# Cross-covariance attention on one core: the Gram norms read before the K^T Q copy, and fp32 transposes in place of fp32 identity matmuls

## The chip, the cores and the metric

The kernel runs on one core of a Trainium2 chip. The metric is the device time of one execution in microseconds (us). The core has five engines that run their own instruction streams and meet at semaphores: TensorE (PE, whose weight loads the profile lists apart as PEld), VectorE (DVE), ScalarE (ACT), GpSimd (POOL) and SyncE (SP, which here only issues DMAs).

## The reference, cut to what matters

```python
# Q, K, V: [8, 12, 512, 64] float32, seeded random
Q_norm = Q / (norm(Q, axis=-2) + 1e-10)       # norm over the 512 rows, per column
K_norm = K / (norm(K, axis=-2) + 1e-10)
attn = einsum('bhnd,bhne->bhde', Q_norm, K_norm)      # 64 x 64 per head
attn = softmax(attn, axis=-1)
out = einsum('bhnd,bhde->bhne', V, attn)
```

For each of the 96 heads, a 64x64 matrix Q^T K is formed, scaled by the column norms of Q and K, put through a softmax, and V is multiplied by its transpose.

## The kernel before

The 96 heads are taken in 24 units of four heads (`HU = 4`). A unit's Q, K and V are tiles of 128 partitions x 1024 floats (512 KB each); head h has the 32 partitions 32h to 32h+31, and each partition holds 16 rows of 64. All loads and stores are issued by SyncE in one queue, in the order of the program.

The scheduling is manual: each engine executes its instructions in the order in which the Python code issues them. The main loop runs over 27 steps `s`, and in a step different pieces work on different units, so that the chain of one unit stretches over four steps:

- `cast_q`, `cast_k` (VectorE, L74 and L77) turn Q and K of unit s+1 to bf16 side by side in `qkb`.
- `grams(s)` (TensorE, L88) multiplies `qkb` with itself: 16 row slices x 4 heads = 64 matmuls of 32 rows, accumulated in `gbuf`, one PSUM bank per head. A head's 128x128 result holds Q^T Q, K^T K and the two cross products.
- `keep_kq(s)` (ScalarE, L93) copies K^T Q (partitions 64 to 127, columns 0 to 63 of each of the four banks) to SBUF.
- `norms(s)` (VectorE, L100) takes the diagonal of each bank with a mask and a sum, four operations; GpSimd (L105) raises the four numbers per partition to the power -1/2, giving `rq`.
- `scale_k(s-1)` (VectorE, L110) scales the rows of K^T Q by the K norms into `kqs`; `logits(s-1)` (TensorE, L116) turns the four 64x64 fp32 blocks by a matmul against the identity; `scale_q(s-1)` (VectorE, L120) scales by the Q norms into `sl`; `exps(s-1)` (ScalarE, L124) and `normalise` (VectorE, L128 to L132, one step later) finish the softmax into a bf16 buffer `ab`.
- `cast_v(s-2)` (ScalarE, L81) and `vtrans(s-2)` (TensorE, L138, eight bf16 transposes; ScalarE copy L140) turn V into `vt`; `doubled(s-2)` (TensorE L145, ScalarE copy L146) puts a second copy of `ab` on the upper partitions.
- `outs(s-3)` (TensorE, L156: 32 matmuls; ScalarE, L160: two copies `so`) forms the output.

Two accesses of one PSUM bank by two engines are put one after the other by the framework: it makes the later one in program order wait for the earlier. So the order of `keep_kq` and `norms`, which read the same four banks, decides which of the two waits. The logits and the doubled attention share one bank as well (`ltile`), and `logits(s-1)` waits for the ScalarE copy of `doubled(s-2)`.

The buffers that matter: `gbuf` is single, so `grams(s+1)` may start when all readers of `grams(s)` are done; `po` has two buffers; Q, K and V tiles have five each. Stores lag by six steps (`STORE_LAG = 6`).

Of the kernel before, what the change touches and what calls it, by code (L numbers as in the profile page):

```python
# [14 lines left out]
D = 64  # L15
# [7 lines left out]
def kernel(  # L23
# [7 lines left out]
    nc = tc.nc  # L31
# [25 lines left out]
    qf, kf, vf, vb, qkb, nsq, rq, kqs, sl, ex, vt, so, kq = ({} for _ in range(13))  # L57
# [55 lines left out]

    def logits(u):
        for h in range(HU):
            nc.tensor.matmul(lg[:, h, :], kqs[u][D:, h, :], ident[D:, D:], tile_position=(D, 0))  # L116

    def scale_q(u):
        s = sl[u] = small.tile([D, HU, D], F32, name="sl")
# [44 lines left out]
    lg = ltile[0:D, 0]  # L164
# [6 lines left out]
    ident = const.tile([128, 128], F32, name="ident")  # L171
# [11 lines left out]
    def on(f, u):  # L183
        if 0 <= u < U:
            f(u)
# [3 lines left out]
    for s in range(U + 3):  # L189
        on(load_qk, s + LOAD_AHEAD)  # L190
        on(load_v, s + V_AHEAD)
        on(store, s - STORE_LAG)
        on(cast_v, s - 2)
        on(cast_q, s + 1)
        on(normalise, s - 2)
        on(scale_k, s - 1)
        on(grams, s)
        on(keep_kq, s)
        on(norms, s)
        on(cast_k, s + 1)  # L200
        on(doubled, s - 2)
        on(outs, s - 3)
        on(logits, s - 1)
        on(scale_q, s - 1)
        on(exps, s - 1)
        on(vtrans, s - 2)
# [32 lines left out]
```

## Time and profile before

| | us |
|---|---|
| median of 3 runs | 146.97 (146.03 to 147.4) |
| the profiled execution, its own time | 146.33 |
| its span, first to last instruction | 144.6 |
| TensorE busy / VectorE busy / ScalarE busy | 105.3 / 93.1 / 99.0 |
| mean granted TensorE clock (1 is full) | 0.767 |

The profile is of one execution. Its parts are: busy time per engine; the span in 40 slices with the clock granted to TensorE and the use of the DMA engines; the DMA queues; the chain of work that ended last, followed back from the last instruction; groups of equal instructions with their mean durations and the idle time ahead of them. In the chain, "issue" is time in which an engine waited for nothing that the profile shows. TensorE records are pipelined, so the duration of one record is longer than the distance to the next.

### The profile page before, as it was taken

The numbers are of one execution on the slowest core, as the hardware profiler recorded it, in microseconds if no ns is written. First come the engines' busy times: TensorE is split into PE (matmuls) and PEld (weight loads), VectorE is DVE, ScalarE is ACT, GpSimd is POOL, SyncE is SP. The second block draws the span as 40 slices with busy tenths as digits, with TensorE's granted clock in tenths as the row PEclk, the third lists the DMA queues.
The fourth block names the chain that finished last, engine by engine and source line by source line (L and its number), as shares of the span: only waits on it lengthen the run. The fifth ranks groups of instructions, "written<-read, shape, count | busy, mean of one in ns | idle before, by whom it ended". The sixth has DMA issues, their size and how long they took to land.

```text
span 144.6 us, 6358 instructions
## 1 busy us (share of the span) xinstructions
PE 105.3 (73%) x2712; PEld 83.4 (58%) x2712; DVE 93.1 (64%) x360; ACT 99.0 (68%) x169; POOL 38.9 (27%) x35
## 2 busy tenths in 40 slices
PE   0347898788999829966496994959699595986630
PEld 0336686566768619754374863848477464965520
DVE  0466979876767766677964777766676975744200
ACT  3011587886687866798866698669497887778960
POOL 6032334313505321413330512320303330320000
PEclk9999999955555985699975589595955998577555
DMA  4999999999999999999999999999999963312333
GB/s 167 402 417 416 404 405 413 399 407 409 416 408 413 419 407 416 413 411 422 406 417 413 415 415 416 419 410 418 411 414 419 381 253 133 150 56 94 145 145 145
DMA packets 13852, 50.73 MB, mean 351 GB/s; under 512 B 1537, under 2 KB 1537, under 8 KB 13825
## 3 DMA queue, kind: packets, MB, share of 16 engines
q1 hardware_dynamic: 13824, 50.34, 86.6%
q8 instruction: 21, 0.34, 1.0%
q14 instruction: 7, 0.05, 0.1%
HBM read 37.75 MB, written 12.58 MB: 348 GB/s over the span
## 4 chain that ended last, share of the span: by engine, by line
PE 56%; DVE 14%; issue 14%; ACT 9%; DMA 3%; ACTq 0%; SPq 0%; DVEq 0%
PE gram L88 23%; PE lgdup L116 11%; PE po L156 10%; PE vps L138 9%; DVE scr L100 6%; PE lgdup L145 4%; DVE qkb L77 4%; DMA kf<-in_K_dram 3%; ACT vb L81 3%; ACT kq L93 2%; ACT vt L140 2%; DVE sl L120 1%; DVE qkb L74 1%; ACT so L160 1%; DVE ab L132 1%
## 5 line engine op out<-in xcount | busy, mean ns | idle before, releaser
L105 POOL TENSOR_TENSOR rq<-nsq,mhalf 128x4 f32<-128x4 f32 x24 | 36.5, 1520 | 89.9 <-DVE nsq L100 89.9
L88 PE MATMUL gram<-qkb 32*128 32x128 bf16 x1536 | 39.7, 270 | 18.7 <-DVE qkb L77 9.3
L88 PEld LDWEIGHTS <-qkb 32*128 32x128 bf16 x1536 | 32.4, 121 | 24.2 <-issue 12.3
L100 DVE CUSTOM_DVE_ANT_0 scr<-gram,ident 128x128 f32<-128x128 f32 x96 | 22.2, 288 | 22.7 <-ACT kq L93 22.6
L160 ACT COPY so<-po 128x512 f32<-128x512 f32 x48 | 26.0, 589 | 6.4 <-PE po L156 5.2
L156 PE MATMUL po<-ab,vt 128*32 128x128 bf16 x768 | 21.1, 264 | 7.5 <-issue 6.3
L156 PEld LDWEIGHTS <-vt 128*32 128x32 bf16 x768 | 15.0, 117 | 17.7 <-issue 8.4
L81 ACT CAST vb<-vf 128x1024 bf16<-128x1024 f32 x24 | 25.1, 1045 | 0.0
L140 ACT COPY vt<-vps 128x1024 bf16<-128x1024 bf16 x24 | 24.0, 1001 | 1.2 <-PE vps L138 0.4
L116 PE MATMUL lgdup<-ident,kqs 64*64 64x64 f32 x192 | 22.3, 279 | 2.6 <-ACT ab L146 2.5
L124 ACT ACTIVATE ex<-sl 64x256 f32<-64x256 f32 x24 | 10.0, 417 | 18.7 <-DVE sl L120 18.7
L116 PEld LDWEIGHTS lgdup<-ident,kqs 64*64 64x64 f32 x192 | 18.4, 184 | 6.7 <-ACT ab L146 4.0
L138 PE MATMUL vps<-identb,vb 128*128 128x128 bf16 x192 | 20.4, 269 | 0.1
L74 DVE CAST qkb<-qf 128x1024 bf16<-128x1024 f32 x24 | 16.3, 677 | 5.0 <-DMA qf<-in_Q_dram 5.0
L93 ACT COPY kq<-gram 64x256 f32<-64x256 f32 x24 | 8.8, 368 | 14.4 <-PE gram L88 13.9
L77 DVE CAST qkb<-kf 128x1024 bf16<-128x1024 f32 x24 | 16.5, 689 | 0.5 <-DMA kf<-in_K_dram 0.5
L138 PEld LDWEIGHTS <-vb 128*128 128x128 bf16 x192 | 14.8, 121 | 2.7 <-issue 0.6
L120 DVE TENSOR_TENSOR sl<-lgdup,rq 64x256 f32<-64x256 f32 x24 | 9.9, 414 | 9.9 <-PE lgdup L116 8.6
L145 PE MATMUL lgdup<-ab,identb 64*64 64x256 bf16 x24 | 8.2, 342 | 5.7 <-DVE ab L132 5.6
L110 DVE TENSOR_TENSOR kqs<-kq,rq 64x256 f32<-64x256 f32 x24 | 10.1, 422 | 1.0 <-POOL rq L105 0.3
L128 DVE TENSOR_REDUCE esum<-ex 64x4 f32<-64x256 f32 x24 | 9.7, 405 | 1.4 <-ACT ex L124 1.4
L132 DVE TENSOR_TENSOR ab<-ex,rinv 64x256 bf16<-64x256 f32 x24 | 10.0, 417 | 0.8
(14 smaller groups left out, 27.6 us busy)
## 6 DMA issues: line engine op xcount, KB each, us to landing
qf<-in_Q_dram SPq DMA_DIRECT2D x24, 512.0 KB, 10.0
kf<-in_K_dram SPq DMA_DIRECT2D x24, 512.0 KB, 10.0
vf<-in_V_dram SPq DMA_DIRECT2D x24, 512.0 KB, 10.1
out_dram<-so SPq DMA_DIRECT2D x24, 512.0 KB, 9.9
```

The lines of the kernel that those rows point to most:

```text
L74: nc.vector.tensor_copy(qkb[u][:, :, 0:D], qf[u])
L77: nc.vector.tensor_copy(qkb[u][:, :, D:], kf[u])
L81: nc.scalar.copy(w.rearrange("p t d -> p (t d)"), vf[u])
L88: nc.tensor.matmul(gbuf[:, h, 0:2 * D], x, x, start=(t == 0), stop=(t == R - 1), tile_position=(NV * h, 0))
L100: nc.vector.tensor_tensor_reduce(out=scr, in0=gbuf[:, h, 0:2 * D], in1=ident, scale=1.0, scalar=1e-20, op0=ALU.mult, op1=ALU.add, accum_ou ...
L105: nc.gpsimd.tensor_tensor(out=r, in0=n2, in1=mhalf, op=ALU.pow)
L116: nc.tensor.matmul(lg[:, h, :], kqs[u][D:, h, :], ident[D:, D:], tile_position=(D, 0))
L138: nc.tensor.transpose(ps[:, t, :], vb[u][:, t, :], identb)
L140: nc.scalar.copy(w, ps)
L145: nc.tensor.matmul(dup[D:], identb[0:D, 0:D], a[0:D, :, 0, :], tile_position=(0, D))
L156: nc.tensor.matmul(po[rows, k, :], vt[u][:, TP // 2 * i + k, rows], a[:, h].rearrange("p a d -> p (a d)"), tile_position=(0, NV * h),)
L160: nc.scalar.copy(s[:, TP // 2 * i:TP // 2 * (i + 1), :], po)
```

## The change

```diff
     def logits(u):
         for h in range(HU):
-            nc.tensor.matmul(lg[:, h, :], kqs[u][D:, h, :], ident[D:, D:], tile_position=(D, 0))
+            nc.tensor.transpose(lg[:, h, :], kqs[u][D:, h, :], ident[D:, D:])
...
         on(grams, s)
-        on(keep_kq, s)
         on(norms, s)
         on(cast_k, s + 1)
         on(doubled, s - 2)
+        on(keep_kq, s)
         on(outs, s - 3)
         on(logits, s - 1)
```

The first hunk gives the four 64x64 turns of a step to TensorE's transpose form: the operands, the place in the array (rows 64 to 127, columns 0 to 63) and the output stay. In the compiled program an fp32 matmul against the identity is two passes, each a weight load and a matmul; a transpose is one. Counted in the compiled programs, TensorE's stream goes from 5,458 instructions to 5,266: eight fewer in each of 24 steps.

The second hunk moves `keep_kq` behind `norms`, `cast_k` and `doubled` in a step. It moves rows on ScalarE alone. In the middle of the program, one step of ScalarE before; `ab_120` is one of the three attention buffers, and the square brackets give the engines waited for:

```order
51 L81 CAST vb<-vf 128x1024 [waits DMAHW2_49,Activation_49]
52 L93 COPY kq<-gram 64x256 [waits PE_49]
53 L146 CAST ab_120<-lgdup 64x4x64 [waits PE_49,Activation_49]
54 L160 COPY so<-po 128x512 [waits PE_49] x2
55 L124 ACTIVATE ex<-sl 64x256 [waits DVE_49]
56 L140 COPY vt<-vps 128x1024 [waits PE_49,Activation_49]
```

And the same step of the changed kernel:

```order
51 L81 CAST vb<-vf 128x1024 [waits DMAHW2_49,Activation_49]
52 L146 CAST ab_120<-lgdup 64x4x64 [waits PE_49,Activation_49]
53 L93 COPY kq<-gram 64x256 [waits DVE_49]
54 L160 COPY so<-po 128x512 [waits PE_49] x2
55 L124 ACTIVATE ex<-sl 64x256 [waits DVE_49]
56 L140 COPY vt<-vps 128x1024 [waits PE_49,Activation_49]
```

The K^T Q copy now stands behind the copy of the doubled attention, and it waits for VectorE's norms in place of TensorE's Gram matmuls. VectorE's rows keep their order; what changes there is the wait of the first norm of a step (one piece of the difference, early in the program):

```order
 L132 TENSOR_TENSOR ab_116<-ex,rinv 64x4x64 [waits DVE_49]
 L110 TENSOR_TENSOR kqs<-kq,rq 64x256 [waits Pool_49]
-L100 ISA scr,nsq<-gram,ident 128x128 [waits Activation_49]
+L100 ISA scr,nsq<-gram,ident 128x128 [waits PE_49]
 L100 ISA nsq 128x1
```

The norms now wait for TensorE alone. TensorE gains a wait: the first Gram matmul of a step now waits for ScalarE, that is for the K^T Q copy of the step before, since that copy is now the last reader of `gbuf`:

```order
 L138 MATMUL vps<-identb,vb 128x128
 L88 LDWEIGHTS qkb [waits DVE_49]
-L88 MATMUL gram<-qkb 128x128
+L88 MATMUL gram<-qkb 128x128 [waits Activation_49]
 L88 LDWEIGHTS qkb
 L88 MATMUL gram<-qkb 128x128
```

The TensorE rows themselves stand in the same order as before.

## The prediction

> **What bounds the kernel now.** I read the page first: the slices and the DMA queues, then the chain by line.
>
> ```profile
> PEclk9999999955555985699975589595955998577555
> DMA  4999999999999999999999999999999963312333
> q8 instruction: 21, 0.34, 1.0%
> PE gram L88 23%; PE lgdup L116 11%; PE po L156 10%; PE vps L138 9%; DVE scr L100 6%; PE lgdup L145 4%; DVE qkb L77 4%; DMA kf<-in_K_dram 3%; ACT vb L81 3%; ACT kq L93 2%; ACT vt L140 2%; DVE sl L120 1%; DVE qkb L74 1%; ACT so L160 1%; DVE a
> ```
>
> The DMA engines are full until about 115 us, yet the waits show that the engines hardly ever wait for data:
>
> ```profile
> DVE qkb L74 <- DMA qf<-in_Q_dram: 5.0, 2, 4.1
> ```
>
> This is the largest wait for a load: two times, 4.1 of its 5.0 us in one of them, at the start. So loads do not set the pace.
>
> Of the span, 14% of the chain is "issue", time in which TensorE waits for nothing that is shown. So I listed the chain in order of time (start, length, what):
>
> ```profile
> 29.28 0.87 PE gram L88 x30
> ...
> 51.93 1.98 issue
> 53.91 0.37 PE po L156 x5
> 54.28 1.04 PE lgdup L116 x8
> 55.32 0.97 PE vps L138 x8
> 56.29 1.82 PE gram L88 x48
> 58.11 0.35 PE lgdup L145
> 58.46 0.98 PE po L156 x29
> ...
> 72.35 0.79 PE gram L88 x42
> ...
> 77.14 1.24 issue
> 78.37 0.93 PE gram L88 x27
> ...
> 115.43 0.97 PE gram L88 x54
> ...
> 118.42 0.56 PE gram L88 x25
> 118.97 1.93 issue
> 120.90 0.73 PE gram L88 x39
> ```
>
> The stops come in the middle of a group of matmuls (after 25 of 64 Gram matmuls, after 27 of 32 output matmuls), where no semaphore stands. The moments at which TensorE **resumes** are what to look at: 29.28, 53.91 (24.63 later, 4 x 6.16), 72.35 (18.44, 3 x 6.15), 78.37 (6.02), 115.43 (37.06, 6 x 6.18), 120.90 (5.47). They beat at about 6.1 us whether the stop is 1.2 or 2.0 us long and whether the clock row stands at 5 or at 9. What lies between two of them is counted by a view of the groups, TensorE alone, from 72.36 to 78.36 us:
>
> ```profile
> L88 PE MATMUL gram<-qkb 32*128 32x128 bf16 x79 | 2.0, 258 | 2.0 <-issue 2.0
> L116 PE MATMUL lgdup<-ident,kqs 64*64 64x64 f32 x8 | 1.1, 318 | 0.0
> L138 PE MATMUL vps<-identb,vb 128*128 128x128 bf16 x8 | 1.0, 311 | 0.0
> L156 PE MATMUL po<-ab,vt 128*32 128x128 bf16 x32 | 0.6, 220 | 0.0
> L145 PE MATMUL lgdup<-ab,identb 64*64 64x256 bf16 x1 | 0.3, 293 | 0.0
> ```
>
> 79 + 8 + 8 + 32 + 1 = 128 matmuls, each with a weight load: 256 instructions. And the DMA queue of the kind "instruction", from 29.28 to 120.90 us:
>
> ```profile
> q8 instruction: 15, 0.25, 1.1%
> ```
>
> 15 packets in 91.62 us, one per **6.11 us**; 0.25 MB / 15 is about 16.7 KB, or 65 bytes for each of 256 instructions. So I read the middle of the program as paced by the supply of TensorE's instructions: a block of 256 every 6.11 us while the data keep the DMA engines full, and TensorE stands still whenever it has used one up.
>
> The Trainium skill, Runtime: NRT & Kernel Launch, section Instruction fetch mechanics, says that an engine's instructions come in 16 KiB blocks of 256, fetched while the current one executes, and that the cost of crossing a boundary is mostly hidden. The trace agrees on the block (256 between two resumptions) and not on the hiding (stops of 1.2 to 2.0 us); by its rule the stops would have another cause, which is the first rival below.
>
> **The change part by part.** The two passes of an fp32 matmul are both instructions of that stream: L116 shows 8 matmuls a step for four calls. A step has 64 Gram matmuls, 8 + 8 + 32 + 1 others, that is 113, as many loads, and one semaphore instruction:
>
> ```profile
> L116 PEldq EVENT_SEMAPHORE  x23: 51/51/51, 16.4 to 131.4; - x23
> ```
>
> Together 227; after the change, 4 + 4 fewer, **219**.
>
> *Up to 120.90 us.* The supply fixes how many instructions TensorE has had by then, so the place in the program tells the gain. At 120.90 TensorE before is 25 matmuls, 50 instructions, into the Gram matmuls of step 22. The logits of steps 1 to 21 are then behind it, 21 x 8 = 168 instructions that the changed program does not have. So it stands at 50 + 168 = 218 of the 219 of step 22: at the end of that step. Before, step 22 ends when the next Gram matmuls begin, at 124.85 (row below). That is **4.0 us** ahead, if TensorE has used up what it had.
>
> Can it? One block earlier, at 115.43, it stands 256 - 218 = 38 instructions ahead of step 22, with seven output matmuls, the logits and the V transposes of step 21 to go, and then a whole step. At the low clock (rows from 54.28 to 58.46) a step is 1.82 + 0.35 + 0.98 + 0.97 plus the logits. No row shows an fp32 transpose. A pass of today costs 1.04 / 8 = 0.13 us there. If a transpose costs a pass, four cost 0.52; if two, nothing is saved; at the pace of the Gram matmuls (64 in 1.89 us by the row of 124.85 below, 0.03) 0.12. I take a pass, the nearest row, and keep 0.12 to 1.04. The low-clock step is then 4.64 us, and from 115.43 it takes 0.2 + 0.52 + 0.97 + 4.64 = 6.3 us, against 5.47 to the next block: 0.8 late. At full clock it is not late. The clock row has both about there; I subtract **0.4**, and 3.6 are left. Further back the same comparison is easy: 219 / 256 x 6.11 = 5.23 us of supply a step against 4.64 of work, so the stops remain and take in everything else that the change saves.
>
> Among it is the move of the copy.
>
> ```profile
> L100 DVE CUSTOM_DVE_ANT_0 scr<-gram,ident 128x128 f32<-128x128 f32 x96 | 22.2, 288 | 22.7 <-ACT kq L93 22.6
> L93 ACT COPY kq<-gram 64x256 f32<-64x256 f32 x24 | 8.8, 368 | 14.4 <-PE gram L88 13.9
> ```
>
> VectorE's norms now wait 22.6 us in all for the copy. They would start some 0.4 us earlier (one copy), and so would GpSimd's power, `cast_k` and `scale_q`. On ScalarE the copy would wait for four norms, 22.2 / 24 = 0.9 us; behind it queue two output copies, the exponential, the copy of V and the cast of V. In place of the copy, 0.9 us of norms pass first, so the output copies come about 0.5 us later; the exponential behind them waited for `scale_q` anyway. The new wait of the Gram matmuls on the copy of the step before is covered too: the copy ends about 0.9 + 0.4 us and the semaphores' delay after the Gram matmuls, and TensorE's own other work takes 2.8 at the low clock (0.35 + 0.98 + 0.52 + 0.97). All this I cost at nothing; without the stops as cover it would be worth up to 0.4 us a step. It may bring the first blocks forward by the same 0.4, which goes into the range.
>
> *After 120.90.* The rest are steps 23 to 26, where DMA is no longer full.
>
> ```profile
> 124.85 1.89 PE L88 MATMUL gram<-qkb 32*128 32x128 bf16 x64
> 132.14 1.11 PE L116 MATMUL lgdup<-ident,kqs 64*64 64x64 f32 x8 [0.31 <-ACT ab L146]
> 133.19 1.04 PE L138 MATMUL vps<-identb,vb 128*128 128x128 bf16 x8
> 134.32 1.01 ACT L140 COPY vt<-vps 128x1024 bf16<-128x1024 bf16 x1
> ```
>
> The last logits start when ScalarE has made its copy, and the V transposes and their copy follow them: half the passes, **0.5 us** earlier. In step 23 ScalarE's queue (cast of V, then `ab`) is late as before, so nothing more is saved there.
>
> Sum: 3.6 + 0.5 = 4.1 us of the profiled execution's own 146.33, giving 142.2. That execution lies 0.64 under the median of 146.97, from which it would be 142.9. I take **142.4**.
>
> The Trainium skill, TensorE: Matmul & The Clock Gate, Part 4 (PE-mode transpose), says that transposes do not count as activity that raises the clock; the clock row is low in nearly half the slices already. By it TensorE would be 0.8 late in place of 0.4, and the sum would be 142.8.
>
> **The rivals.**
>
> *Supply does not pace it.* The stops would stay as they are, or be something that goes by work, and what the chain loses would count in full: half of the 11% of L116 (8.0 us) and the 2% of the K^T Q copy (2.9): 135.4. For it: both are on the chain. Against it: the even beat and the count of 256. The Trainium skill's rule on hidden fetches, named above, would lead here.
>
> *Nothing is saved in the stream.* If the transposes come as two passes each, the blocks end where they do now and only crumbs of the tail move: 145.8 to 146.5. Against it is the count of the compiled program, 192 instructions fewer.
>
> *Slower: the transposes do not overlap.* The page's groups give the whole length of one record:
>
> ```profile
> L116 PE MATMUL lgdup<-ident,kqs 64*64 64x64 f32 x192 | 22.3, 279 | 2.6 <-ACT ab L146 2.5
> L116 PEld LDWEIGHTS lgdup<-ident,kqs 64*64 64x64 f32 x192 | 18.4, 184 | 6.7 <-ACT ab L146 4.0
> ```
>
> If an fp32 transpose let nothing run beside its load and its matmul, four would take 4 x (0.279 + 0.184) = 1.85 us, and a low-clock step 4.12 + 1.85 = 5.97, over today's supply of 227 / 256 x 6.11 = 5.42 a step. It decides from 1.30 us for the four. With half of some 21 steps at the low clock, 0.55 x 10.5 = 5.8 us more: 152. Against it: the two passes of today overlap (0.13 us apart for records of 0.28), and the eight bf16 transposes of V do.
>
> **How the numbers follow.** Forecast 0.77, supply not the pace 0.08, nothing saved 0.09, slower 0.06. Within the forecast the ends are 5.4 us (not late: 4.0; first blocks early: 0.4; four transposes of the tail at 0.12 in place of 1.11: 1.0) and 1.7 (4.0 less 0.8 late and less a beat 0.1 us longer over 15 blocks, no gain in the tail): 140.9 to 144.6 from the profiled execution, 145.3 from the median. To leave out no more than 2 in 10 the range takes in half of "nothing saved" and a little towards the first rival: 140.0 to 145.9. About 1% (1.5 us) is what a measurement here can tell from no change. Faster 0.85, within 1% 0.09, slower 0.06.
>
> **What would show it.** L116 with 96 matmuls and 96 loads in place of 192; 20 packets in the instruction queue in place of 21; stops still in the middle of groups, resuming every 6.0 to 6.3 us with 256 instructions between; the wait of the norms for the copy gone, in its place a wait of the copy for the norms on ScalarE; K^T Q copies about 5.2 us apart in the middle. It is wrong if the resumptions drift apart or vanish, if "issue" falls from the chain, or if the four transposes of a step take more than about a microsecond.

## The result and the profile after

| | before | after |
|---|---|---|
| median of the runs, us | 146.7 | 142.15 (142.0 to 143.02) |
| profiled execution, own time / span, us | 146.33 / 144.6 | 142.27 / 140.5 |
| TensorE / VectorE / ScalarE busy, us | 105.3 / 93.1 / 99.0 | 95.7 / 93.9 / 99.2 |

The ratio is 0.970 (95% interval 0.964 to 0.976). On a second chip it was 0.974 (0.969 to 0.979).

From the page of the changed kernel, the DMA and instruction-queue rows, the chain by line and three groups (operation, tiles, shape and count | busy us in all, mean ns of one | idle us ahead of it and what ended most of that):

```profile
DMA  4999999999999999999999999999999998223333
q8 instruction: 20, 0.33, 0.9%
PE gram L88 15%; DMA vf<-in_V_dram 12%; PE po L156 9%; PE vps L138 8%; PE lgdup L116 6%; ACT so L160 5%; ACT vb L81 4%; DVE scr L100 3%; PE lgdup L145 3%; DVE ab L132 2%; DVE esum L128 2%; ACT ex L124 2%; ACT vt L140 1%; ACT ab L146 1%; DVE
L100 DVE CUSTOM_DVE_ANT_0 scr<-gram,ident 128x128 f32<-128x128 f32 x96 | 22.2, 287 | 11.6 <-PE gram L88 11.3
L93 ACT COPY kq<-gram 64x256 f32<-64x256 f32 x24 | 8.8, 368 | 16.6 <-DVE nsq L100 16.4
L116 PE MATMUL lgdup<-ident,kqs 64*64 64x64 f32 x96 | 12.9, 273 | 2.4 <-ACT ab L146 2.4
```

L116 has 96 records where it had 192, and the instruction queue moved 20 packets, not 21. The norms' wait for the copy (22.6 us) is gone; the copy waits for the norms instead, 16.4 us. And the DMA row is full for 32 of the 40 slices where it was for 31: the loads and the compute end closer together.

The chain in order of time, TensorE's stops and what followed:

```profile
53.09 1.86 issue
54.94 0.89 PE gram L88 x49
...
59.56 1.67 issue
61.23 0.62 PE gram L88 x31
...
65.62 1.91 issue
67.53 0.51 PE gram L88 x12
...
114.00 1.92 issue
115.91 0.29 PE po L156 x7
```

The stops are still there, as long as before, and their ends keep the beat: 54.94, 61.23 (6.29 later), 67.53 (6.30), 115.91 (48.38, 8 x 6.05). What lies between two of them, from 61.24 to 67.52 us, TensorE alone:

```profile
L88 PE MATMUL gram<-qkb 32*128 32x128 bf16 x83 | 2.2, 273 | 1.7 <-issue 1.7
L138 PE MATMUL vps<-identb,vb 128*128 128x128 bf16 x8 | 1.0, 311 | 0.0
L156 PE MATMUL po<-ab,vt 128*32 128x128 bf16 x32 | 0.6, 220 | 0.0
L116 PE MATMUL lgdup<-ident,kqs 64*64 64x64 f32 x4 | 0.6, 281 | 0.0
L145 PE MATMUL lgdup<-ab,identb 64*64 64x256 bf16 x1 | 0.3, 293 | 0.0
```

83 + 8 + 32 + 4 + 1 = 128 matmuls and as many loads: 256 instructions again, but four fewer pairs of them are logits, so a block reaches further into the program. Where the time came from is read in one row of the timeline, the first Gram matmul of step 23:

```profile
121.18 1.07 PE L88 MATMUL gram<-qkb 32*128 32x128 bf16 x64
```

In the kernel before, the same matmul started at 124.85. Of the 4.1 us of span, 3.67 are gained by there and 0.43 in the steps after.

### The profile page after: what moved, and what is told of

Its sections match the earlier page's. It is cut to its first block, busy times and chain, and to the rows that moved or that the text cites. A ratio compares the mean times of both kernels' runs of the same rounds, so it can differ in the third digit from the quotient of the medians.

```text
span 140.5 us, 6167 instructions
## 1 busy us (share of the span) xinstructions
PE 95.7 (68%) x2616; PEld 73.1 (52%) x2616; DVE 93.9 (67%) x360; ACT 99.2 (71%) x169; POOL 40.1 (29%) x35
## 4 chain that ended last, share of the span: by engine, by line
PE 40%; issue 17%; ACT 14%; DMA 12%; DVE 11%; SPq 2%; ACTq 0%; DVEq 0%
PE gram L88 15%; DMA vf<-in_V_dram 12%; PE po L156 9%; PE vps L138 8%; PE lgdup L116 6%; ACT so L160 5%; ACT vb L81 4%; DVE scr L100 3%; PE lgdup L145 3%; DVE ab L132 2%; DVE esum L128 2%; ACT ex L124 2%; ACT vt L140 1%; ACT ab L146 1%; DVE qkb L74 1%
## 5 line engine op out<-in xcount | busy, mean ns | idle before, releaser
L105 POOL TENSOR_TENSOR rq<-nsq,mhalf 128x4 f32<-128x4 f32 x24 | 37.7, 1569 | 84.8 <-DVE nsq L100 84.8
L88 PE MATMUL gram<-qkb 32*128 32x128 bf16 x1536 | 39.1, 269 | 22.4 <-issue 13.0
L156 PE MATMUL po<-ab,vt 128*32 128x128 bf16 x768 | 21.8, 268 | 7.9 <-issue 6.8
L93 ACT COPY kq<-gram 64x256 f32<-64x256 f32 x24 | 8.8, 368 | 16.6 <-DVE nsq L100 16.4
L146 ACT CAST ab<-lgdup 64x256 bf16<-64x256 f32 x24 | 8.8, 368 | 10.6 <-PE lgdup L145 10.2
L116 PE MATMUL lgdup<-ident,kqs 64*64 64x64 f32 x96 | 12.9, 273 | 2.4 <-ACT ab L146 2.4
L116 PEld LDWEIGHTS lgdup<-ident,kqs 64*64 64x64 f32 x96 | 7.9, 135 | 6.5 <-ACT ab L146 3.8
```

Source lines behind the costliest of these rows:

```text
L88: nc.tensor.matmul(gbuf[:, h, 0:2 * D], x, x, start=(t == 0), stop=(t == R - 1), tile_position=(NV * h, 0))
L105: nc.gpsimd.tensor_tensor(out=r, in0=n2, in1=mhalf, op=ALU.pow)
L116: nc.tensor.transpose(lg[:, h, :], kqs[u][D:, h, :], ident[D:, D:])
L156: nc.tensor.matmul(po[rows, k, :], vt[u][:, TP // 2 * i + k, rows], a[:, h].rearrange("p a d -> p (a d)"), tile_position=(0, NV * h),)
```

## Experiments

The theory in all of them: in the middle of the program TensorE gets 256 instructions every 6.1 us, because the data keep the DMA engines full; so instructions count, and work beside them does not. The main rival: the work on the chain counts.

**One part alone: the order.** The logits are fp32 matmuls again.

```diff
 # the changed kernel, with
-            nc.tensor.transpose(lg[:, h, :], kqs[u][D:, h, :], ident[D:, D:])
+            nc.tensor.matmul(lg[:, h, :], kqs[u][D:, h, :], ident[D:, D:], tile_position=(D, 0))
```

> Only the copy of K^T Q moved behind the norms; the logits stay fp32 matmuls, so TensorE's stream keeps its 5,458 instructions. Theory (the supply of TensorE's instructions paces the middle of the program): the stops take up what the earlier norms save, so 146.3 us, at most 0.7 under the kernel before; resumptions every 6.1 us as before; the norms' 22.6 us of waiting for the copy gone. Rival (the work on the chain counts): the copy's 2% of the chain comes off, 143.5 to 144.

Measured: 146.31 against 146.25 us, ratio 1.001 (0.998 to 1.005). The waits of that kernel, and its chain, show what the rival leaves out (engine, line and what it waited for: us in total, times, longest):

```profile
DVE scr L100 <- PE gram L88: 11.4, 12, 2.0
PEld L88 <- issue: 15.0, 19, 2.8
```

The norms no longer wait for the copy at all; they wait for the Gram matmuls, and those wait for instructions (12.3 us in the kernel before, 15.0 now). The stops end at

```profile
72.36 0.79 PE gram L88 x42
...
78.38 0.57 PE gram L88 x27
...
84.40 0.58 PE gram L88 x12
```

They are 6.02 us apart. The time is as expected, 2 us and more over the rival's range. An earlier norm alone is worth nothing here: it is taken up by the stop.

**The other part alone: the transposes.** The copy stays ahead of the norms; this kernel ran twice, on two chips.

```diff
 # the kernel before, with
-            nc.tensor.matmul(lg[:, h, :], kqs[u][D:, h, :], ident[D:, D:], tile_position=(D, 0))
+            nc.tensor.transpose(lg[:, h, :], kqs[u][D:, h, :], ident[D:, D:])
```

> Only the logits turned by fp32 transposes (5,266 TensorE instructions); the copy stays ahead of the norms. Theory: nearly the whole gain, 142 to 143 us. Rival (work on the chain counts, and the two parts share the gain): the transposes alone leave out what the order gives, 143.5 to 144.5.

> The changed kernel once more, beside the transposes alone on one chip. 0.970 of the kernel before, that is some 4.2 us less.

> The transposes alone once more (the copy of K^T Q stays ahead of the norms), to settle what the order adds beside them: alone it gave nothing, yet the transposes alone gave 2.8 us and both together 4.5 against other runs. Theory: while supply binds the order is covered, so it can only add where supply no longer binds, in the last steps (0.25 us a step for some five steps): 0.7 to 1.5 us over the changed kernel. Rival (the two parts do not depend on each other): no difference beyond what the order gave alone, 0 to 0.3 us.

Measured: 143.49 us, 0.983 (0.978 to 0.987), and again 143.45, 0.983 (0.979 to 0.987), beside 142.3 for the whole change on that second chip, 0.974 (0.969 to 0.979). So the transposes give most of the gain, and the order, worth nothing alone, adds 1.15 us on top of them. The first expectation took the order at under half a microsecond, and missed: 143.49 lies at the edge of its rival's range (143.5 to 144.5), by which the two parts share the gain. The second had the size (0.7 to 1.5) but, by the profile, not the place. The first long stop in the middle of Gram matmuls, of the transposes alone (second chip) and of the whole change:

```profile
28.39 0.90 PE gram L88 x50
29.29 2.26 issue
31.55 0.40 PE gram L88 x14
```

```profile
26.69 0.83 PE gram L88 x50
27.52 2.57 issue
30.09 0.41 PE gram L88 x14
```

The same instruction ends the stop at 31.55 us without the order (30.83 in the other profile) and at 30.09 with it (30.05 in the other), after 50 of 64 matmuls in both. The beat then keeps this distance (the table two experiments further on follows it to 117 us). So by these four profiles the earlier norms act through the moment at which the first blocks come, ahead of the stretch that supply paces. Why the blocks there come when they do is not settled: in the kernel before, with the slower order, the same instruction came at 29.28, and the order alone (29.49) did not bring it forward.

**The instructions given back, without the work.** Four tiny matmuls a step are added to the changed kernel.

```diff
 # the changed kernel, at the end of grams(u)
+        for i in range(4):
+            nc.tensor.matmul(gbuf[0:NV, 0, 256:257], qkb[u][0:NV, 0, 0:NV], qkb[u][0:NV, 0, 0:1], start=True, stop=True, tile_position=(0, 0))
```

> The changed kernel with four more tiny bf16 matmuls a step (32 x 32 weights, one column, into an unused column of the Gram bank), each with its weight load: TensorE's stream is back at 5,458 instructions, with hardly any work added (at the pace of the Gram matmuls, 0.03 us each, 0.1 us a step). Theory: the gain goes, 145.5 to 146.5 us, with 256 instructions between resumptions 6.1 us apart. Rival (passes of work count): 142.2 to 143.

Measured: 145.59 us, 0.997 of the kernel before (0.994 to 1.000), that is 3.4 us over the changed kernel's 142.15 by runs on different chips, or 2.3 to 2.7% by the ratios (to 0.974 and 0.970). Four columns a step cost nearly all that the change had given, and the ends of the stops keep the beat (start, us of it, engine, line and count; L90 are the four tiny matmuls):

```profile
73.58 1.46 PE gram L88 x43
75.04 0.19 PE gram L90 x4
...
79.61 1.04 PE gram L88 x30
...
85.62 0.69 PE gram L88 x17
```

They are 6.03 and 6.01 us apart. The tiny matmuls are not free, though: the four take 0.19 us here, more than the 0.1 that was expected, and 2.4% of the chain in all, some 3.5 us. At that price the rival would have nearly the same total, so the time of this run alone does not decide between count and work. The next run and the beat do.

**More work in the same instructions.** 15 of 16 Gram matmuls run over 160 columns.

```diff
 # the changed kernel, in grams(u)
+                n = 2 * D if t == R - 1 else 2 * D + 32
+                y = qkb[u].rearrange("p t d -> p (t d)")[NV * h:NV * (h + 1), 2 * D * t:2 * D * t + n]
-                nc.tensor.matmul(gbuf[:, h, 0:2 * D], x, x, start=(t == 0), stop=(t == R - 1), tile_position=(NV * h, 0))
+                nc.tensor.matmul(gbuf[:, h, 0:n], x, y, start=(t == 0), stop=(t == R - 1), tile_position=(NV * h, 0))
```

> The changed kernel with more work in the same number of instructions: 15 of 16 Gram matmuls of a head run over 160 columns in place of 128 (the extra 32 go to an unused part of the bank). The Gram matmuls take 23% longer where columns set their pace: 0.25 to 0.45 us a step. Theory: the stops take it up while supply binds, and only the steps after it show it: 142 to 144 us. Rival (work on the chain counts): 6 to 10 us more, 148 to 152.

Measured: 143.34 us, 0.982 (0.975 to 0.989). The extra columns cost 1.2 us by the medians (0.8 to 1.2% by the ratios), not 6 to 10. They are work all the same, by the Gram group here and in the second profile of the changed kernel, whose granted clocks are close (0.829 and 0.815):

```profile
L90 PE MATMUL gram<-qkb 32*128 32x160 bf16 (+1 forms) x1536 | 43.0, 275 | 22.4 <-issue 12.2
L88 PE MATMUL gram<-qkb 32*128 32x128 bf16 x1536 | 36.5, 258 | 21.5 <-issue 12.0
```

6.5 us more of TensorE's time in the same instructions cost 1.2 us; the tiny matmuls, with about half as much time in instructions of their own, cost 3.4. The beat says it more directly. The same two places in TensorE's stream, its 478th and its 2262nd matmul, are 14 blocks apart, and all profiles of kernels with 64 Gram matmuls a step and all their loads have them so (us):

| | 478th starts | 2262nd starts | between | from there to the end |
|---|---|---|---|---|
| before | 29.28 | 115.43 | 86.15 | 29.1 |
| the order alone | 29.49 | 114.81 | 85.32 | 29.2 |
| the transposes alone, two profiles | 30.83, 31.55 | 116.67, 117.38 | 85.84, 85.83 | 24.5, 24.7 |
| both (the change), two profiles | 30.09, 30.05 | 115.91, 115.71 | 85.82, 85.66 | 24.6, 24.8 |
| both, with the tiny matmuls | 30.48 | 115.95 | 85.47 | 28.0 |
| both, with wide Gram matmuls | 31.71 | 117.27 | 85.56 | 25.3 |

The 14 blocks take 85.3 to 86.2 us whatever work is in them. The kernels differ in when the paced stretch begins and in how much of the program is left when it ends. So most of what the wide columns cost (1.6 of 2.1 us between the two profiled executions) stands ahead of the paced stretch, and not in the last steps, as was expected.

**The data taken off the DMA engines.** V is loaded for three units only and used again, so the output is that of other V; once in the changed kernel, once in the kernel before.

```diff
 # load_v(u)
-        vf[u] = vp.tile([128, R * D], F32, name="vf")
+        if u >= 3:
+            vf[u] = vf[u % 3]
+            return
+        vf[u] = const.tile([128, R * D], F32, name=f"vf{u}")
```

> The changed kernel without most of its V loads: V is loaded for the first three units only and used again for the others (the output is that of other V). TensorE's 5,266 instructions and all other work stay. Theory (a block of instructions takes 6.1 us only because the data keep the DMA engines full): with 3 in place of 4 transfers a step the DMA engines have gaps, blocks come in time, the stops shrink or go, and the pace is that of ScalarE and of TensorE at the low clock, 4.4 to 4.8 us a step: 128 to 134 us. Rival (the block time is fixed, or the stops have another cause): 141 to 142.

> The same removal of V loads from the kernel before. It shows what the change's saving of work is worth when supply does not bind. Theory: stops gone; the loop through the K^T Q copy, the norms and ScalarE takes 4.6 us a step at full clock, TensorE 5.2 at the low one: 133 to 138, that is 3 to 5 us over the changed kernel without those loads. Rival (fixed block time): 145 to 147.

Measured: 136.15 us (133.96 to 136.96) and 140.1 us (137.9 to 140.88). Both miss by the median (128 to 134 and 133 to 138 were expected) and lie some 5 us under their rivals' ranges; their distance, 3.95 us, is inside the 3 to 5. The runs of these two spread over 2%, so I go by the spacing of steps in their profiles (executions of 136.96 and 140.12 us) rather than by the ratio. From 104 to 116 us the changed kernel's queues show

```profile
q1 hardware_dynamic: 416, 1.51, 31.5%
q8 instruction: 3, 0.05, 1.8%
```

With the data at 31.5% of the DMA engines, three blocks came in 12 us, as many as TensorE used, and there is no stop. The trace places the single packets of the instruction queue (the queue view over narrow windows finds them), and they show where the time of a block goes. In the changed kernel with all its loads, from 30 to 114 us, the next packet starts 3.6 to 3.8 us after TensorE has entered a block, takes 1.0 to 1.1 us, and the block that it brings begins 1.3 to 1.6 us after its end: together the beat. Without most V loads, in the three blocks entered from 99 to 110 us, it starts 0.7 to 1.1 us after. So what the data add is the wait ahead of the packet. A step there is what the softmax loop through VectorE and ScalarE takes. The chain of the changed kernel and then the timeline of the kernel before, both at `ab`, the last operation of `normalise`:

```profile
104.02 0.42 DVE ab L135
...
108.34 0.42 DVE ab L135
...
112.66 0.42 DVE ab L135
```

```profile
105.96 0.42 DVE L135 TENSOR_TENSOR ab<-ex,rinv 64x256 bf16<-64x256 f32 x1
110.54 0.42 DVE L135 TENSOR_TENSOR ab<-ex,rinv 64x256 bf16<-64x256 f32 x1
115.12 0.42 DVE L135 TENSOR_TENSOR ab<-ex,rinv 64x256 bf16<-64x256 f32 x1
```

4.32 us a step against 4.58. In the chains of both, no TensorE row stands in this loop: in the changed kernel it runs over the scaling of K^T Q, the norms, the output copy, the exponential and the softmax's sum; in the kernel before over the K^T Q copy (107.11 and again 111.69 us), the norms, the scaling, the exponential, the copy of V^T and the cast of V. So where supply does not bind, the change is worth 0.26 us a step there, by its order and not by its instruction count as far as the chains tell; no run takes the two parts apart without the V loads, and 0.26 us a step is only part of the 3.95. The whole times missed because the stops stay longer than was expected. In the changed kernel without these loads the DMA row is still nearly full up to slice 28, that is 95 us,

```profile
DMA  4999999999999999969799999999542143413333
```

and its last stop, of 2.03 us, ends at 95.03.

**Far fewer instructions.** Q and K loaded so that a head lies on 128 partitions, in runs of 1 KB, for Gram matmuls of 128 rows; and on 64 partitions, in runs of 2 KB, for 64 rows.

```diff
 # the changed kernel, 128 rows
+    Qf, Kf = (x.rearrange("b h n d -> (b h n d)").rearrange("(u h p f) -> u p h f", h=HU, p=128, f=R // HU * D) for x in (Q, K))
 ... (the two loads follow)
-        for t in range(R):
+        for t in range(R // HU):
             for h in range(HU):
-                x = qkb[u][NV * h:NV * (h + 1), t, :]
+                x = qkb[u][:, h * (R // HU) + t, :]
 ... (the matmul, on 128 rows)
```

> The changed kernel with Q and K loaded so that each head has all 128 partitions (4 rows of 64 each, runs of 1 KB in place of 4 KB): 16 Gram matmuls of 128 rows a step in place of 64 of 32 rows; TensorE's stream falls to 2,962 instructions, 123 a step. Theory: 123/256 x 6.1 = 2.9 us of supply a step no longer binds; no stops; the pace is then that of the loads (about 5.0 us a step by the spacing of the DMA issues) and of ScalarE (4.1 us busy a step): 129 to 134 us. If the shorter runs slow the loads, up to 138. Rival (work counts): 16 passes at 0.08 to 0.13 us are 1.2 to 2.1 us a step against 1.1 to 1.9 now, so 141 to 143.

```diff
 # the changed kernel, 64 rows
+    Qf, Kf = (x.rearrange("b h n d -> (b h n d)").rearrange("(u g q f) -> u q g f", g=2, q=128, f=R // 2 * D) for x in (Q, K))
 ... (the two loads follow)
-        for t in range(R):
+        for t in range(R // 2):
             for h in range(HU):
-                x = qkb[u][NV * h:NV * (h + 1), t, :]
+                x = qkb[u][D * (h % 2):D * (h % 2 + 1), R // 2 * (h // 2) + t, :]
 ... (the matmul, on 64 rows)
```

> The changed kernel with Q and K in runs of 2 KB: a head on 64 partitions with 8 rows each, 32 Gram matmuls of 64 rows a step (3,730 TensorE instructions, 155 a step). Theory: supply 155/256 x 6.1 = 3.7 us a step, no stops; the loads bind, at a rate between that of 4 KB runs (5.0 us a step) and of 1 KB runs (some 5.5): 132 to 139 us. Rival (work on the chain counts): 141 to 143.

Measured: 143.19 us, 0.982 (0.976 to 0.987), for 128 rows, a clear miss, beside its rival's 141 to 143 but not for the rival's reason; 137.66 us, 0.942 (0.937 to 0.948), for 64 rows, as expected. The 128-row kernel's page and its largest wait for data:

```profile
GB/s 147 300 350 353 366 370 368 370 364 367 367 383 383 394 390 383 396 392 383 399 395 388 400 394 392 397 395 393 396 395 392 393 390 416 413 406 297 159 149 149
DMA 63%; ACT 15%; SPq 6%; DVE 6%; PE 4%; issue 3%; ACTq 0%
ACT vb L82 <- DMA vf<-in_V_dram: 21.2, 17, 2.3
```

The stops are gone, as the theory has it: "issue" is 3% of the chain, after 17% in the changed kernel. What was wrong is the size of the next bound. The data moved at 350 to 400 GB/s for most of the span where runs of 4 KB move at about 410, and ScalarE waited 17 times for V. With runs of 2 KB:

```profile
DMA  4999999999999999999999999999999999996333
DMA 69%; ACT 11%; DVE 8%; issue 3%; PE 3%; SPq 2%; ACTq 0%
ACT vb L83 <- DMA vf<-in_V_dram: 16.5, 15, 2.2
```

Supply is out of the way at less loss of rate, and the loads are most of the chain (DMA 69%).

**A faster version than both.** Since the loads bind there and stores stand ahead of the last loads in SyncE's queue, the stores were put three steps later; and, to keep most runs at 4 KB, a second kernel takes the 64-row form in every third unit only.

```diff
-    STORE_LAG = 6
+    STORE_LAG = 9
 ...
-    sop = ctx.enter_context(tc.tile_pool(name="sop", bufs=10))
+    sop = ctx.enter_context(tc.tile_pool(name="sop", bufs=13))
```

> The kernel with 64-row Gram matmuls, its stores issued nine steps behind in place of six (and 13 output buffers). Theory: there the loads bind, and the last V load is issued at 111.7 us behind all stores that stand ahead of it; three stores later means three transfers (1.26 us each) fewer ahead of it, 3 to 3.8 us less: 134 to 135 us. Rival (ScalarE's and VectorE's work binds): 137 to 138.

> The same store lag, with 64-row Gram matmuls and 2 KB runs in every third unit only (4,754 TensorE instructions, 198 a step on average). Theory: supply, 198/256 x 6.1 = 4.7 us a step, is just under the 5.0 of the loads in 4 KB runs, so the loads bind at nearly their best rate: 132.5 to 134.5, under the kernel with 64 rows throughout. Rival (a third is not enough, since a long unit still takes 219 instructions): stops return, 136 to 139.

Measured: 133.73 us, 0.917 (0.913 to 0.921), and 134.07 us, 0.919 (0.915 to 0.924). The first came out just under what was expected, the second inside it; both are 6% under the changed kernel. In the mixed kernel the stops are back, which its rival had said, without the cost that it had named (L102 are the Gram matmuls of the units with 4 KB runs, L170 output matmuls):

```profile
PEld L102 <- issue: 6.5, 8, 2.1
PE po L170 <- issue: 5.0, 3, 2.5
ACT vb L91 <- DMA vf<-in_V_dram: 2.6, 1, 2.6
```

That the mixed kernel would be the faster one, as its expectation had it, is not shown: its median is the higher one, and the intervals overlap.

## Why the prediction was right

The mechanism was right: TensorE's instruction supply paces the middle, and the transposes save instructions of it. That the total came out so close is in part luck, since errors cancelled in two places. Step by step, against the profile after:

- *The stretch that supply paces.* Step 23 begins at 121.18 us, where the kernel before had 124.85: 3.67 us, forecast 3.6. Here two errors of about half a microsecond cancelled. The block that the forecast took to begin at 115.43 came at 115.91 (the allowance was for 0.4 earlier). From there TensorE reached step 23 in 5.27 us, in part at full clock and without a stop, where the forecast had 5.47 for the next block and 0.4 for being late.
- *The beat.* 6.0 to 6.3 us from stop to stop, with 256 instructions, unchanged. The table shows it independent of the work, the missing V loads that full DMA engines are needed for it.
- *The transposes.* One pass each: 0.56 us on the chain for the four at the low clock, forecast 0.52.
- *The order at nothing.* Right alone (ratio 1.001) and not right beside the transposes, where it gave 1.15 us by an earlier first stop. The forecast had set up to 0.4 us aside for that, in the range and not in the sum. By its sum the transposes alone would have given the whole 4.1; they gave 2.4 to 2.8. With them alone the paced stretch begins 1.6 to 2.3 us later than before (30.83 and 31.55 against 29.28) and ends 1.2 to 2.0 later (116.67 and 117.38 against 115.43), which is about what is missing. The forecast had no term for such a delay, and with the order beside them most of it is gone. That the two cancel and leave 4.1 is luck, and the cause of the delay stays open.
- *The rest.* From the start of step 23 to the end 19.75 us before and 19.32 after: 0.43, forecast 0.5. From the start of the last logits to the end it is 12.46 and 11.97, the half of the passes that the forecast named; but in the kernel after it was the output matmuls, and no longer ScalarE's copy, that came last ahead of those logits.
- *Own time.* 146.33 - 142.27 = 4.06, forecast 4.1.

One reading of the prediction was too broad: the 14% of "issue" on the chain are not TensorE's alone. Of some 20 us about 16 stand ahead of TensorE's rows, the others ahead of ScalarE's and VectorE's.

The rivals fall with it: the work on the chain (135.4) by the measured 142.15, the even 14 blocks and the wide Gram matmuls; nothing saved by the 96 records; slow transposes by the 0.56 us. Whether transposes raise the clock can be told neither way: it was 0.767 on average before and 0.76 and 0.815 in the two profiles after.

## What to carry to other kernels

Stops of an engine in the middle of a run of equal instructions, with nothing that it waits for, are worth counting: if their ends keep an even beat and the same number of instructions lies between, the engine is likely to be short of instructions. Two things helped here: fewer of them, and fewer data on the DMA engines meanwhile. Adding instructions and adding work are two different tests of it, and the added instructions bring some work of their own. Then ask which bound comes next before saving more; here fewer instructions by runs of 1 KB gave back part of the gain (0.982 against 0.970), and a middle way, runs of 2 KB, gave nearly twice the change's (0.942). A part that is worth nothing alone (the order) can still be worth something beside another, so each is tried both ways.

## What the runs showed of the hardware

With the DMA engines full, a block of 256 TensorE instructions took 6.0 to 6.3 us, 14 of them 85.3 to 86.2 us in eight profiles; with them at about a third, three came in 12 us without a stop. In the changed kernel the packet that brings a block started 3.6 to 3.8 us after TensorE had entered the block ahead of it, with the DMA engines full, and 0.7 to 1.1 us after, with them at about a third. With Q and K in runs of 1 KB the data moved at 350 to 400 GB/s, with all in runs of 4 KB at about 410. An fp32 transpose of 64 x 64 was recorded as one load and one matmul where the fp32 matmul had two of each, and four took 0.56 us at a granted clock of 0.50, where the eight passes of four fp32 matmuls took 1.04.
